# Two token halves chunk by chunk, the tail of a recurrence around a gate's products, and weights split four chunks ahead, in a kernel of eight stages

## The chip, the cores and the metric

The kernel runs on one core of a Trainium2 chip. The metric is the device time of one execution in microseconds (us). Before the change the median of three runs is 1450.25 us (1450.15 to 1452.18). The core's engines work side by side, each through its own list of instructions: TensorE (PE) multiplies matrices, VectorE (DVE), ScalarE (ACT) and GpSimd (POOL) work on tiles of 128 partitions, SyncE (SP) issues most of the transfers.

## The reference

256 tokens of 1024 features pass through two equal layers, each with three branches, and then through a pooling mixer, two convolutional feed-forward stages, two small embedding stages and a sparse attention. The change is in the two layers. One of them, cut to what matters (all in float32):

```python
h = rmsnorm(x, pre_norm_g[l])
proj = h @ w_in[l]
(u, v, z_a, c_q, c_kv, k_rope, z_b, x_c, z_c, g_a, g_b, g_c) = jnp.split(proj, cuts, axis=-1)
y_a = gmlp_spatial(u, v, ...) * jax.nn.silu(z_a)
y_b = mla_attention(c_q, c_kv, k_rope, ...) * jax.nn.silu(z_b)
y_c = rg_lru(x_c, ...) * jax.nn.silu(z_c)
merged = (jax.nn.sigmoid(g_a) * (y_a @ w_proj_a[l])
          + jax.nn.sigmoid(g_b) * (y_b @ w_proj_b[l])
          + jax.nn.sigmoid(g_c) * (y_c @ w_proj_c[l]))
x = x + rmsnorm(merged @ w_out[l], post_norm_g[l])
```

The recurrence of the third branch, `rg_lru`, over 1280 channels:

```python
a = jnp.exp(log_a)
mult = jnp.sqrt(jnp.maximum(1.0 - jnp.exp(2.0 * log_a), 0.0))
bterm = mult * (i * xc)          # h[t] = a[t] * h[t-1] + bterm[t], a scan over the tokens
```

## The kernel before, in words

**Products.** Every float32 product of matrices is made of three: each operand is split into a high part (hi) and a low part (lo), and `mm3` issues hi by hi (line 481), hi by lo (482) and lo by hi (483). Two shapes matter. Where the output is by tokens, the stationary operand is a slice of the activations and the weights stream, 512 columns at a time, for the two halves of 128 tokens one after the other (`tok_halves`, `tok_group`, `tok_pair`). Where it is by features (`feat_tile`, `feat_pair`), 256 tokens stream.

**Weights.** `Stream` (from line 342) brings the weights of the whole program in one sequence of chunks of up to 128 x 1024. SyncE loads a chunk into one of 4 raw buffers, ScalarE copies it to hi (line 376), VectorE subtracts to lo (line 379, in two pieces of 512 columns), and there are 7 buffers for hi and 7 for lo. `get` hands out the next chunk and, by two numbers given at line 428, first writes the loads of the next three chunks and the splits of the next two. A buffer is free again once the last product that reads it is done.

**One layer.** The hidden activations hT are normalised and transposed. The gMLP branch (u, v, za), the attention (c, zb) and the recurrence's input (xc) come first. Then the gates and projections: `gate` makes two halves of 512 columns and takes their tanh on ScalarE into tmp (line 898); `project` makes the product of a branch's y with its projection and adds it to merged on VectorE (lines 907 and 908). `gates` computes the recurrence's decay av (five tiles of 128 x 512, ending in an exponential on ScalarE at line 973) and multiplies its input xc (line 968).

**The tail of the recurrence**, lines 980 to 993: first both column blocks of the third gate (gc 0 and gc 1), then for each of the five tiles the square of av and its minimum with 1 on VectorE (lines 985, 986) and the square root on ScalarE (987), then xc times that (989) and the scan over the tokens (992), two scans for each tile. After it come zc's products, and for each of its five pairs a silu (lines 617 and 618), the product with av (1001) and the split into yc (491 on ScalarE for the high part, 492 on VectorE for the low part). pc's products need yc: for each column block n, half 0 goes through all ten slices of yc, then half 1 does. merged is transposed into ms, multiplied with the output weights (`tok_pair`), normalised (sums of squares as "junk" at 512, ms at 501, rs on GpSimd at 502), and added to x half by half (lines 1016 and 1020); the next stage's norm follows in each half at once (tmp at 526, then transposes, or, at the pool mixer, products with pm at 1089).

**What sets the order.** The code is not a list of each engine's instructions: a scheduler places every instruction on its engine by the order in which it was written and by when buffers come free. An engine then works through its list strictly in that order. So a split that is written earlier can come to stand ahead of an instruction that it has nothing to do with.

Of the kernel before, what the change touches and what calls it, by code (L numbers as in the profile page):

```python
# [418 lines left out]
class Net:  # L419
    def __init__(self, tc, ctx, aps, out):  # L420
        self.tc, self.nc = tc, tc.nc
        self.aps, self.out = aps, out
        self.cp = ctx.enter_context(tc.tile_pool(name="const", bufs=1))
        self.sp = ctx.enter_context(tc.tile_pool(name="stream", bufs=1))
        self.ap = ctx.enter_context(tc.tile_pool(name="acts", bufs=1))
        self.tp = ctx.enter_context(tc.tile_pool(name="temps", bufs=2))
        self.psp = ctx.enter_context(tc.tile_pool(name="psum", bufs=4, space=bass.MemoryType.PSUM))
        self.w = Stream(self.nc, aps["w"], self.sp, 3, 2)

# [136 lines left out]
    def tok_group(self, key, f, N=512, kts=KD, kper=2):  # L566
        return list(self.tok_halves(key, f, N, kts, kper))

# [164 lines left out]
    def first_layer(self, l):  # L733
# [160 lines left out]
        def gate(gk, n):  # L894
            ts = []
            for ps in self.tok_halves((gk, l, n), hT):
                ts.append(self.tmp())
                nc.scalar.activation(ts[-1], ps, AF.Tanh, scale=0.5)
            return ts

        def project(pk, n, y, kts, ts, first=False):
            for half, ps in enumerate(self.tok_halves((pk, l, n), y, kts=kts)):
                mg, t = merged[half][n], ts[half]
# [71 lines left out]
        for kind, i in MERGE_ORDER:  # L975
            if kind == "a":
                project("pa", i, ya, 8, gate("ga", i))
            else:
                gates(i)
        tg = [gate("gc", n) for n in range(2)]  # L980
        tv = self.u2s("tv", 5)
        quarter = self.small(1, "quarter", 2)
        nc.vector.tensor_scalar(quarter, av[4][:, :1], 0.0, 0.25, op0=ALU.mult, op1=ALU.add)
        for j in range(5):
            nc.vector.tensor_tensor(tv[j], av[j], av[j], op=ALU.mult)
            nc.vector.tensor_scalar(tv[j], tv[j], 1.0, None, op0=ALU.min)
            nc.scalar.activation(tv[j], tv[j], AF.Sqrt, bias=quarter, scale=-0.25)
        for j in range(5):
            nc.vector.tensor_tensor(xc[j], xc[j], tv[j], op=ALU.mult)
            for e in range(2):  # L990
                ct = 2 * j + e
                nc.vector.tensor_tensor_scan(ctile(av, ct), ctile(av, ct), ctile(xc, ct), 0.0,  # L992
                                             op0=ALU.mult, op1=ALU.add)
        if l == 1:
            self.ple_load(0)
            self.w.scale = self.row("pscale")
# [8 lines left out]
        for n in range(2):  # L1005
            project("pc", n, yc, KL, tg[n])
        for n in range(2):
# [525 lines left out]
```

## Time and profile before

| | |
|---|---|
| median of three runs | 1450.25 us |
| the profiled execution | 1449.2 us, its span 1447.4 us |
| TensorE busy | 1406.5 us, 97% of the span |
| VectorE busy | 1059.7 us, 73% |
| ScalarE busy | 842.0 us, 58% |
| GpSimd busy | 73.2 us, 5% |
| mean granted TensorE clock | 0.996 of full speed |

The span goes from the first to the last instruction of the profiled execution; 1.8 us of its time lie around the span. Times in the rows further down are in us from the span's start. A row of a timeline has start, duration, engine, line, operation, result and operands, and in square brackets how long the engine had been idle before it and what ended that. Products are pipelined: each is recorded longer than the distance to the next one, so for TensorE the distance between starts is what counts.

### The profile page before, as it was taken

To read this page: it belongs to the slowest core of one execution; us is meant where nothing else is said; L and a number is where in the kernel's file an instruction comes from. 1 tells how busy PE (TensorE), PEld (TensorE's weight loads), DVE (VectorE), ACT (ScalarE), POOL (GpSimd) and SP (SyncE) were. 2 spreads that over 40 slices of the span, in tenths; PEclk is the share of its full clock that TensorE was granted. 3 is DMA by queue.
4 is the path that set the end of the run, shared out by engine and by line. 5 is a ranking of instruction groups with operands and counts; after the bars stand their busy time and mean duration, and the time that the engine had idled before them with its cause. 6 is when DMAs were issued, how large, how long until landed. Compare 5 with 4: busy or idle time off the path is not lost.

```text
span 1447.4 us, 23030 instructions
## 1 busy us (share of the span) xinstructions
PE 1406.5 (97%) x8522; PEld 1235.7 (85%) x8522; DVE 1059.7 (73%) x2163; ACT 842.0 (58%) x1411; POOL 73.2 (5%) x118
## 2 busy tenths in 40 slices
PE   6999999999999999999999999999999999999997
PEld 6987889889789878898897899999778677999986
DVE  7856748659677567486597788776795888787765
ACT  6665545656465665456564566554665786665553
POOL 1000002100010000021000000000100120000000
PEclk9999999999999999999999999999999999999999
DMA  8563456554655634555656455555453106655552
GB/s 281 182 195 117 166 183 196 170 202 149 218 161 195 197 117 159 190 187 170 211 178 218 150 201 178 190 186 193 167 181 131 59 15 191 194 184 189 187 162 90
DMA packets 73408, 249.32 MB, mean 172 GB/s; under 512 B 8272, under 2 KB 8912, under 8 KB 73296
## 3 DMA queue, kind: packets, MB, share of 16 engines
q1 hardware_dynamic: 72576, 245.95, 51.9%
q10 hardware_dynamic: 720, 1.91, 0.4%
q8 instruction: 67, 1.10, 0.3%
q14 instruction: 45, 0.37, 0.1%
HBM read 246.77 MB, written 1.05 MB: 171 GB/s over the span
## 4 chain that ended last, share of the span: by engine, by line
PE 81%; DVE 9%; DMA 4%; ACT 3%; issue 2%; POOL 1%; POOLq 0%; ACTq 0%; DVEq 0%; SPq 0%
PE psA L481 22%; PE psA L482 22%; PE psA L483 22%; DMA raw<-in_w_dram 3%; PE psB L481 3%; PE psB L482 3%; PE psB L483 3%; DVE lo L379 3%; ACT hi L376 2%; PE psB L538 1%; DVE av L992 1%; POOL rs L502 1%; PE psB L1036 1%; PE psB L1054 1%; PE psB L1422 1%
## 5 line engine op out<-in xcount | busy, mean ns | idle before, releaser
L379 DVE TENSOR_TENSOR lo<-raw,hi 128x512 fp32r<-128x512 f32 (+2 forms) x897 | 583.9, 677 | 217.4 <-ACT hi L376 212.0
L376 ACT ACTIVATE hi<-raw 128x1024 fp32r<-128x1024 f32 (+3 forms) x449 | 466.7, 1044 | 310.6 <-PE psA L483 110.3
L482 PE MATMUL psA<-hT,hi 128*128 128x256 f32 x1160 | 328.6, 283 | 0.5 <-DVE hT L489 0.5
L483 PE MATMUL psA<-hT,lo 128*128 128x256 f32 x1160 | 328.2, 283 | 0.0
L481 PE MATMUL psA<-hT,hi 128*128 128x256 f32 x1160 | 328.2, 283 | 0.0
L481 PE MATMUL psA<-hi,hT 128*128 128x512 f32 (+2 forms) x592 | 230.5, 390 | 3.9 <-ACT hT L488 3.9
L482 PE MATMUL psA<-lo,hT 128*128 128x512 f32 (+2 forms) x592 | 228.6, 386 | 1.6 <-DVE lo L379 1.6
L483 PE MATMUL psA<-hi,hT 128*128 128x512 f32 (+2 forms) x592 | 229.1, 388 | 0.0
L482 PEld LDWEIGHTS psA<-hT,hi 128*128 128x128 f32 x1160 | 221.9, 191 | 2.0 <-DVE hT L489 0.7
L481 PEld LDWEIGHTS psA<-hT,hi 128*128 128x128 f32 x1160 | 221.8, 191 | 1.5 <-ACT hT L488 0.2
L483 PEld LDWEIGHTS psA<-hT,lo 128*128 128x128 f32 x1160 | 222.0, 191 | 0.0
L481 PEld LDWEIGHTS psA<-hi,hT 128*128 128x128 f32 x592 | 111.5, 188 | 24.1 <-ACT hT L488 4.9
L482 PEld LDWEIGHTS psA<-lo,hT 128*128 128x128 f32 x592 | 111.4, 188 | 21.9 <-DVE lo L379 2.3
L483 PEld LDWEIGHTS psA<-hi,hT 128*128 128x128 f32 x592 | 111.4, 188 | 20.6 <-DVE hT L489 0.7
L1135 DVE SCALAR_TENSOR_TENSOR tmp<-psA,colt,tmp 128x255 f32<-128x255 f32 (+1 forms) x176 | 84.1, 478 | 1.2
L502 POOL TENSOR_TENSOR rs<-ms,mhalf 128x1 f32<-128x1 f32 x34 | 28.9, 851 | 979.2 <-DVE ms L501 790.6
L481 PE MATMUL psB<-hi,fact 128*128 128x512 f32 x176 | 68.8, 391 | 0.0
L482 PE MATMUL psB<-lo,fact 128*128 128x512 f32 x176 | 68.8, 391 | 0.0
L483 PE MATMUL psB<-hi,fact 128*128 128x512 f32 x176 | 68.5, 389 | 0.0
L1132 ACT ACTIVATE tmp<-psA,colt 128x256 f32<-128x256 f32 x88 | 48.5, 551 | 1.9
L512 ACT ACTIVATE junk<-x 128x512 bf16<-128x512 f32 x36 | 22.6, 628 | 36.3 <-DVE x L1165 14.0
L936 POOL CAST es<-xs 64x256 fp32r<-64x256 f32 x48 | 29.4, 640 | 270.1 <-ACT xs L488 269.3
(343 smaller groups left out, 2235.0 us busy)
## 6 DMA issues: line engine op xcount, KB each, us to landing
raw<-in_w_dram SPq DMA_DIRECT2D x414, 512.0 KB, 3.7
raw<-in_w_dram SPq DMA_DIRECT2D x24, 384.0 KB, 3.9
row<-in_rows_dram SPq DMA_DIRECT2D x34, 256.0 KB, 5.6
raw<-in_w_dram SPq DMA_DIRECT2D x8, 448.0 KB, 3.2
raw<-in_w_dram SPq DMA_DIRECT2D x4, 480.0 KB, 3.3
x<-in_x_dram SPq DMA_DIRECT2D x4, 256.0 KB, 4.6
pm<-in_pm_dram ACTq DMA_DIRECT2D x2, 512.0 KB, 5.3
out_dram<-h SPq DMA_DIRECT2D x4, 256.0 KB, 2.1
```

Of the source, the lines that this page charges most:

```text
L376: self.nc.scalar.activation(hi[:, :n], t[:, :n], AF.Copy)
L379: self.nc.vector.tensor_tensor(lo[:, c], t[:, c], hi[:, c].bitcast(F32), op=ALU.subtract)
L481: mm(ps, a[0], b[0], start=start, stop=False)
L482: mm(ps, a[0], b[1], start=False, stop=False)
L483: mm(ps, a[1], b[0], start=False, stop=stop)
L502: nc.gpsimd.tensor_tensor(rs, ms, self.mhalf, op=ALU.pow)
L512: nc.scalar.activation(junk[:, :s.shape[1]], s, AF.Square, scale=float(n) ** -0.5 / mul, accum_out=ss[:, i:i + 1])
L538: nc.tensor.transpose(ps[:, i, :], src[:, (done + i) * P:(done + i + 1) * P], self.cf("ident"))
L936: nc.gpsimd.tensor_copy(edges[p][m][i][r], xs.pair(ct)[i][r].bitcast(F32))
L992: nc.vector.tensor_tensor_scan(ctile(av, ct), ctile(av, ct), ctile(xc, ct), 0.0, op0=ALU.mult, op1=ALU.add)
L1132: nc.scalar.activation(dst, src, AF.Identity, bias=self.col("fb", ct, l), scale=self.col("fw", 2 * 2 * KF + ct, l))
L1135: nc.vector.scalar_tensor_tensor(dst[:, s:], src[:, :S - s], self.col("fw", (2 - s) * 2 * KF + ct, l), dst[:, s:], op0=ALU.mult, op1=ALU.add)
```

## The change

The diff has four parts. `Stream` gets 6 and 4 in place of 3 and 2. `tok_group`, which was a list of what `tok_halves` yields, now takes a chunk of weights, does its products for half 0 and for half 1, and only then takes the next; both sums are complete at the end. `gate` uses it, and so does `project`, except for pc's second column block. And the tail of the recurrence is written anew: squares on ScalarE, minima on GpSimd, square roots, then gc 0, then products and scans, then gc 1.

```diff
-        self.w = Stream(self.nc, aps["w"], self.sp, 3, 2)
+        self.w = Stream(self.nc, aps["w"], self.sp, 6, 4)
...
     def tok_group(self, key, f, N=512, kts=KD, kper=2):
-        return list(self.tok_halves(key, f, N, kts, kper))
+        ps = [self.psA(), self.psA()]
+        for c in range(-(-kts // kper)):
+            wh, wl = self.w.get((*key, c), N)
+            for half in range(2):
+                for kg in range(c * kper, min(kts, (c + 1) * kper)):
+                    k = kg % kper
+                    self.mm3(ps[half][:, :N], f.pair(kg, half), (wh[:, k, :], wl[:, k, :]), kg == 0, kg == kts - 1)
+        return ps
...
         def gate(gk, n):
             ts = []
-            for ps in self.tok_halves((gk, l, n), hT):
+            for ps in self.tok_group((gk, l, n), hT):
...
-        def project(pk, n, y, kts, ts, first=False):
-            for half, ps in enumerate(self.tok_halves((pk, l, n), y, kts=kts)):
+        def project(pk, n, y, kts, ts, first=False, last=False):
+            for half, ps in enumerate((self.tok_halves if last else self.tok_group)((pk, l, n), y, kts=kts)):
...
-        tg = [gate("gc", n) for n in range(2)]
         tv = self.u2s("tv", 5)
         quarter = self.small(1, "quarter", 2)
         nc.vector.tensor_scalar(quarter, av[4][:, :1], 0.0, 0.25, op0=ALU.mult, op1=ALU.add)
         for j in range(5):
-            nc.vector.tensor_tensor(tv[j], av[j], av[j], op=ALU.mult)
-            nc.vector.tensor_scalar(tv[j], tv[j], 1.0, None, op0=ALU.min)
+            nc.scalar.activation(tv[j], av[j], AF.Square)
+            nc.gpsimd.tensor_scalar(tv[j], tv[j], 1.0, 1.0, op0=ALU.min, op1=ALU.mult)
+        for j in range(5):
             nc.scalar.activation(tv[j], tv[j], AF.Sqrt, bias=quarter, scale=-0.25)
+        tg = [gate("gc", 0)]
         for j in range(5):
             nc.vector.tensor_tensor(xc[j], xc[j], tv[j], op=ALU.mult)
             for e in range(2):
...
+        tg.append(gate("gc", 1))
...
         for n in range(2):
-            project("pc", n, yc, KL, tg[n])
+            project("pc", n, yc, KL, tg[n], last=(n == 1))
```

All lines from 566 on move down by 7, those behind the tail by 9: line 618 of before is 625 of after, 1016 is 1025.

The order in which engines get their instructions changes with it at three places. The first is ScalarE in layer 0, from the gates of the recurrence to the first silu of zc. Before (tmp at 967 are the gates' last tanh, at 898 the third gate's, tv at 987 the square roots):

```order
L967 ACTIVATE tmp<-psA,lrub_717 128x256 x3
L376 ACTIVATE hi<-raw 128x1024 x2
L898 ACTIVATE tmp<-psA 128x512
L376 ACTIVATE hi<-raw 128x1024 x3
L898 ACTIVATE tmp<-psA 128x512
...
L987 ACT_TABLE_LOAD
L987 ACTIVATE tv<-tv,quarter 128x512 x5
```

and now (squares at 991, square roots at 994, the third gate's tanh at 905):

```order
L974 ACTIVATE tmp<-psA,lrub_733 128x256 x3
L991 ACTIVATE tv<-av 128x512 x5
L994 ACT_TABLE_LOAD
L994 ACTIVATE tv<-tv,quarter 128x512 x5
L376 ACTIVATE hi<-raw 128x1024 x3
L905 ACT_TABLE_LOAD
L905 ACTIVATE tmp<-psA 128x512 x2
L376 ACTIVATE hi<-raw 128x1024 x4
```

The square roots have moved ahead of the third gate's tanh, and three splits that stood ahead of that tanh now stand behind the square roots.

The second is VectorE in the same stretch, from the last xc of the gates on. Before (the tail is lines 985 to 992; a scan is listed as an operation of av and xc):

```order
L968 SCALAR_TENSOR_TENSOR xc<-tmp,xc 128x256 x3
L379 TENSOR_TENSOR lo<-raw,hi 128x512 x18
L985 TENSOR_TENSOR tv<-av 128x512 x2
L986 TENSOR_SCALAR tv<-tv 128x512 x2
...
L989 TENSOR_TENSOR xc<-xc,tv 128x512 x2
L992 SCALAR_TENSOR_TENSOR av<-av,xc 128x256 x4
L618 SCALAR_TENSOR_TENSOR tmp<-tmp,psA 128x512
```

and now (products at 997, scans at 1000):

```order
L975 SCALAR_TENSOR_TENSOR xc<-tmp,xc 128x256 x3
L379 TENSOR_TENSOR lo<-raw,hi 128x512
L997 TENSOR_TENSOR xc<-xc,tv 128x512 x2
L1000 SCALAR_TENSOR_TENSOR av<-av,xc 128x256 x4
L997 TENSOR_TENSOR xc<-xc,tv 128x512 x2
L379 TENSOR_TENSOR lo<-raw,hi 128x512 x6
L1000 SCALAR_TENSOR_TENSOR av<-av,xc 128x256 x4
L997 TENSOR_TENSOR xc<-xc,tv 128x512
L379 TENSOR_TENSOR lo<-raw,hi 128x512
L1000 SCALAR_TENSOR_TENSOR av<-av,xc 128x256 x2
L379 TENSOR_TENSOR lo<-raw,hi 128x512 x16
L625 SCALAR_TENSOR_TENSOR tmp<-tmp,psA 128x512
```

The 18 splits that stood ahead of the tail now mostly stand behind it, and none of its squares and minima is left.

The third is VectorE at the end of layer 1, where x is updated half by half (x_70 is half 0, x_71 half 1), and the pool mixer's rows are scaled (tmp). Before:

```order
L501 TENSOR_SCALAR ms<-ss 128x1
L1020 SCALAR_TENSOR_TENSOR x_70<-t,rs,x_70 128x512 x2
L501 TENSOR_SCALAR ms<-ss 128x1
L526 SCALAR_TENSOR_TENSOR tmp<-x_70,rs,row 128x512 x2
L1016 TENSOR_TENSOR t<-psA,row 128x512 x2
```

and now:

```order
L501 TENSOR_SCALAR ms<-ss 128x1
L1029 SCALAR_TENSOR_TENSOR x_70<-t,rs,x_70 128x512
L379 TENSOR_TENSOR lo<-raw,hi 128x512 x4
L1029 SCALAR_TENSOR_TENSOR x_70<-t,rs,x_70 128x512
L501 TENSOR_SCALAR ms<-ss 128x1
L526 SCALAR_TENSOR_TENSOR tmp<-x_70,rs,row 128x512 x2
L1025 TENSOR_TENSOR t<-psA,row 128x512 x2
```

Four splits have come between the two updates of half 0. On TensorE the order at the three places is the same as before, but for the order of halves within a product.

## Rows read from the trace of the kernel before

**Rows 1.** The page's first part: busy time of each engine, its share of the span, and instructions.

```profile
PE 1406.5 (97%) x8522; PEld 1235.7 (85%) x8522; DVE 1059.7 (73%) x2163; ACT 842.0 (58%) x1411; POOL 73.2 (5%) x118
```

**Rows 2.** The waits of TensorE over the whole span: the operation that waited, what it waited for, us in total, times, the longest.

```profile
PE psB L538 <- DVE tmp L526: 12.6, 5, 9.6
...
PE psA L481 <- ACT yc L491: 3.3, 3, 1.7
...
PE psA L482 <- DVE lo L379: 1.6, 2, 1.3
...
PE psA L483 <- DVE yc L492: 0.8, 2, 0.4
```

**Rows 3.** The timeline of TensorE in layer 0, at pc's first product and at the end of the first half's eighth slice.

```profile
356.57 0.40 PE L481 MATMUL psA<-hi,yc 128*128 128x512 f32 x1
...
361.58 0.39 PE L482 MATMUL psA<-lo,yc 128*128 128x512 f32 x1
361.81 0.39 PE L483 MATMUL psA<-hi,yc 128*128 128x512 f32 x1
363.85 0.50 PE L481 MATMUL psA<-hi,yc 128*128 128x512 f32 x1 [1.66 <-ACT yc L491]
364.19 0.40 PE L482 MATMUL psA<-lo,yc 128*128 128x512 f32 x1
365.00 0.50 PE L483 MATMUL psA<-hi,yc 128*128 128x512 f32 x1 [0.41 <-DVE yc L492]
```

**Rows 4.** The same in layer 1; of the stretch from 758.13 to 767.90 only the ends and the place between its two parts.

```profile
755.61 0.40 PE L481 MATMUL psA<-hi,yc 128*128 128x512 f32 x1
...
758.13 0.39 PE L483 MATMUL psA<-hi,yc 128*128 128x512 f32 x1
...
763.56 0.57 PE L481 MATMUL psA<-hi,yc 128*128 128x512 f32 x1
...
767.90 0.39 PE L481 MATMUL psA<-hi,yc 128*128 128x512 f32 x1
```

**Rows 5.** Windows of the span: length, then busy us and instructions of PE, PEld, DVE, ACT, POOL, then the granted TensorE clock, the share of the DMA engines, GB/s.

```profile
764.00:767.00 3.00, 3.00 (x9) 2.33 (x8) 1.66 (x3) 0.63 (x1) 0.00 (x0) 0.50 0.77 264
...
822.00:825.00 3.00, 3.00 (x15) 3.00 (x16) 2.66 (x5) 1.16 (x3) 0.00 (x0) 0.50 0.88 261
```

**Rows 6.** The timeline of VectorE in layer 0, in the recurrence's tail and behind it.

```profile
328.36 1.29 DVE L985 TENSOR_TENSOR tv<-av 128x512 f32<-128x512 f32 x2
329.57 0.76 DVE L986 TENSOR_SCALAR tv<-tv 128x512 f32<-128x512 f32 x2
...
339.56 2.42 DVE L992 TENSOR_TENSOR_SCAN av<-av,xc 128x256 f32<-128x256 f32 x4
341.91 0.65 DVE L618 SCALAR_TENSOR_TENSOR tmp<-tmp,psA 128x512 f32<-128x512 f32 x1
...
364.26 0.68 DVE L492 SCALAR_TENSOR_TENSOR yc<-tmp,yc 128x512 fp32r<-128x512 f32 x1
```

**Rows 7.** The timeline of ScalarE in the same stretch: the table load ahead of the square roots, and one of the splits among the silus.

```profile
329.54 1.28 ACT L987 ACT_TABLE_LOAD   x1
...
346.59 1.06 ACT L376 ACTIVATE hi<-raw 128x1024 fp32r<-128x1024 f32 x1 [1.61 <-DMA raw<-in_w_dram]
```

**Rows 8.** The timeline of VectorE in layer 1: the low part of yc's fifth pair.

```profile
765.66 0.69 DVE L492 SCALAR_TENSOR_TENSOR yc<-tmp,yc 128x512 fp32r<-128x512 f32 x1 [0.70 <-ACT yc L491]
```

**Rows 9.** The timeline of VectorE in layer 0's gMLP branch: the last steps of v's norm.

```profile
115.10 1.30 DVE L869 TENSOR_TENSOR sv<-sv,row 128x512 f32<-128x512 f32 x2
116.32 1.28 DVE L870 TENSOR_TENSOR sv<-sv,row 128x512 f32<-128x512 f32 x2
```

**Rows 10.** The timeline of TensorE there: the products that read them.

```profile
122.84 1.46 PE L873 MATMUL psB<-sv,wsT 128*128 128x256 f32 x6
```

**Rows 11.** The timeline of ScalarE in layer 0: the last tanh of the recurrence's gates.

```profile
306.36 1.21 ACT L967 ACTIVATE tmp<-psA,lrub 128x256 f32<-128x256 f32 x3
```

**Rows 12.** The page's groups of instructions: the squares that ScalarE does for the norms; count, busy us, mean ns of one, idle time before.

```profile
L512 ACT ACTIVATE junk<-x 128x512 bf16<-128x512 f32 x36 | 22.6, 628 | 36.3 <-DVE x L1165 14.0
```

**Rows 13.** GpSimd's instructions by line and shape: count, busy us, mean ns of one, idle time before and what ended it.

```profile
L1412 POOL TENSOR_SCALAR es<-es,sm 128x256 f32<-128x256 f32 x16 | 8.5, 550 | 24.7 <-PE psB L1422 8.0 <-DVE sm L1408 7.9 <-PE psA L1399 6.2
L1412 POOL TENSOR_SCALAR es<-es,sm 128x128 f32<-128x128 f32 x16 | 6.2, 403 | 95.8 <-DVE sm L1408 95.8
```

**Rows 14.** The timeline of VectorE in layer 0, during gc 0 and gc 1.

```profile
314.11 4.02 DVE L379 TENSOR_TENSOR lo<-raw,hi 128x512 fp32r<-128x512 f32 x6 [2.89 <-ACT hi L376]
...
325.04 3.41 DVE L379 TENSOR_TENSOR lo<-raw,hi 128x512 fp32r<-128x512 f32 x5 [5.07 <-ACT hi L376]
```

**Rows 15.** The timeline of VectorE at the end of layer 1.

```profile
809.05 1.42 DVE L1020 SCALAR_TENSOR_TENSOR x<-t,rs,x 128x512 f32<-128x512 f32 x2 [0.73 <-POOL rs L502]
811.31 0.21 DVE L501 TENSOR_SCALAR ms<-ss 128x1 f32<-128x1 f32 x1 [0.85 <-ACT junk L512]
812.19 1.42 DVE L526 SCALAR_TENSOR_TENSOR tmp<-x,rs,row 128x512 f32<-128x512 f32 x2 [0.66 <-POOL rs L502]
...
820.96 1.41 DVE L526 SCALAR_TENSOR_TENSOR tmp<-x,rs,row 128x512 f32<-128x512 f32 x2 [0.45 <-POOL rs L502]
```

**Rows 16.** The timeline of TensorE there: the pool mixer's products for half 1.

```profile
821.76 2.93 PE L1089 MATMUL psB<-pm,tmp 128*128 128x128 f32 x12 [2.71 <-DVE tmp L526]
```

**Rows 17.** The waits of TensorE from 366 to 430 us, at the step from layer 0 to layer 1.

```profile
PE psB L538 <- DVE tmp L526: 1.2, 2, 0.8
```

## The prediction

> **What bounds the kernel now.** I read the page's busy line first, then TensorE's waits, then the timelines around the places where the diff works, and the order of instructions last. TensorE is busy for 1406.5 of the span's 1447.4 us [rows 1], so only what shortens its waits or lifts its clock can shorten the run: nothing in the diff adds or takes away a matrix product. The list of its waits [rows 2] splits them by what came last. Weights are a small part: the wait for a low part of a split weight (DVE lo) is 1.6 us in all, 1.3 of it in one piece. What can be won by a change to the first layers is the wait for yc: 3.3 us for its high part, 0.8 for its low part. The largest entry, 12.6, is mostly one wait of 9.6 us at the start, which the diff doesn't touch.
>
> The reader should see the place of the yc wait in the two timelines. In layer 0 [rows 3] products of 512 columns start every 0.227 us (361.58, 361.81, and 24 of them from 356.57 on); then come 2.04, 0.34 and 0.81 us instead of three times 0.227: 3.19 - 0.68 = 2.5 us lost. In layer 1 [rows 4] ten steps from 758.13 to 763.56 take 5.43 instead of 2.27: 3.2 us lost. Right after it the granted clock of 764 to 767 is 0.50, the lower of the two levels [rows 5]. There the twelve steps from 763.56 to 767.90 take 4.34 instead of 2.72: 1.6 us more. Together **7.3 us** hang on yc in the two layers.
>
> Why is yc late? In layer 0, pc's first product starts at 356.57, and half 0 runs through eight of its ten slices before it needs the fifth pair, 24 x 0.227 = 5.4 us later. The fifth pair's low part starts on VectorE at 364.26. Ahead of it stands VectorE's tail of the recurrence: from 328.36 to 341.9 it does squares, minima, products and scans without one lo among them, and the silu of the first pair waits until 341.91 [rows 6].
>
> **Part 1, products chunk by chunk (tok_group).** For pc with n = 0 both halves of a chunk now run together: the fifth pair is wanted after 48 products instead of 24, 10.9 us after the start instead of 5.4. In layer 0 that is 367.5, against 364.94 at which the low part was done even in the kernel before [rows 6]; 2.5 us to spare. In layer 1 pc starts at 755.61 [rows 4], so the pair is wanted at 766.5; its low part ended at 765.66 + 0.69 = 766.35 [rows 8], 0.15 us to spare. So this part alone already removes the wait of layer 0 and nearly that of layer 1: -2.5 and -3.2, and, with no wait ahead of it, I take the 1.6 of slow clock with them. What it costs: half 0's sums come 5.4 us later than before, together with half 1's. For the gates that is free, since their tanh is used only by project. In the gMLP branch the normalised v must be there for the products with wsT: VectorE has it at 116.32 + 1.28 = 117.6, TensorE starts at 122.84 [rows 9, 10], 5.2 us later. The second half's chain, some 3 to 4 us of VectorE work (four of 0.64 in the same rows, and the statistics), now follows the first's instead of lying 5.4 us behind it; it still fits. I take 0, with 0 to +2 for each layer as bounds.
>
> **Part 2, the recurrence's tail.** Five multiplications of 0.60 and five minima of 0.34 [rows 6] leave VectorE, 4.7 us; the rest of the tail moves ahead, between gate 0's and gate 1's products. Who is loaded instead? ScalarE's last tanh of the gates ends at 307.57 [rows 11]. Five squares of 512 columns: the nearest row, the same function, is 0.63 us each with about 0.53 from start to start [rows 12], so they end near 310.2; the table load of 1.28 [rows 7] ends at 311.5. GpSimd has no 512-column row. The same operation takes 403 ns at 128 columns and 550 at 256 [rows 13]: 147 ns for each 128 more gives 0.84 us. Bounds are 0.55 (no more than at 256) and 1.5 (some way beyond twice the longer row, 1.1). With 0.84 the last minimum ends at 308.1 + 4.2 = 312.3, the last square root near 314.3. VectorE had two holes there, 2.9 us before 314.11 and 5.1 before 325.04 [rows 14]; the products and scans (five of 0.6, ten of 0.59, 8.9 us) now lie around them. What must not be late is the second chunk of gate 1, wanted at about 319.7 (gate 0 ends at 316.9, one chunk is 2.7): its hi now stands behind the five square roots, and its lo behind four products and four scans. I get its lo at about 318.4, 1.3 us to spare. So no wait, and the recurrence ends near 325 instead of 341.9. That makes the fifth yc ready some 3.5 to 5 us after zc instead of 8.5, which widens part 1's spare to 5 us and covers layer 1. No further term: the 7.3 are not won twice.
>
> The Trainium skill speaks against the move: ScalarE: Activation LUTs, "Rules for kernel authors", wants mul and min on VectorE, which it puts at up to about three times faster per element in bf16. By that a square would be 3 x 0.60 = 1.8 us, an estimate from that page, the five would end at 316.5, gate 1's second chunk would come some 0.4 us late in each layer, and the forecast would be 0.8 us higher. The float rows here are 0.63 against 0.68 [rows 6, 12], so I don't take it.
>
> **Part 3, weights four ahead (6, 4).** The order shows the limit: seven hi and lo buffers and four raw ones. Ahead of zc's first silu ScalarE has issued only three more hi than before. With 1.6 us of weight waits in the whole run [rows 2]: 0, bounds -0.3 and +0.5. But the splits are now written earlier, so the scheduler puts them elsewhere among the norm chains, and there VectorE pays.
>
> At the step from layer 1 to the pool mixer, VectorE's two updates of x for half 0 were one group at 809.05; ms follows at 811.31, the scaled rows (tmp) at 812.19, then half 1's t and x, and its tmp at 820.96 [rows 15]. TensorE waits for that last tmp, 2.71 us until 821.76 [rows 16]. In the new order four lo stand between the two updates, 4 x 0.60 = 2.4 us, and ScalarE has two hi ahead of half 0's sums of squares. Everything in half 0's chain is one behind the other, with 0.85 and 0.66 us of idle time that wait on its own links, so the delay runs through: half 1's t, which VectorE takes only after half 0's tmp, comes 2.4 later, and so does the wait's end. TensorE has no other work in its order there: **+2.3**. Bounds: 0, if the lo fall into VectorE's idle time, and +3.8, if TensorE then runs 3 us longer at the lower level, as it does after this wait now (822 to 825 at 0.50, [rows 5]), which costs another 1.5. At the step between the layers two more lo come ahead of half 0's ms in the same way; there the transposes waited 1.2 us in two pieces for tmp [rows 17]. +0.3, bounds -0.5 and +1.2.
>
> **The sum.** -2.5 - 3.2 - 1.6 + 2.3 + 0.3 = -4.7 us. The profiled run took 1449.2 us (span 1447.4, 1.8 around it): 1444.5. The median of the three runs is 1450.25, 1.05 above the profiled one; the forecast in that measure is **1445.5**, 0.3% faster. Own range 1443.0 to 1447.5. A measurement of this kernel tells about 0.2%, 2.9 us, from no change.
>
> **Rivals.**
> A, nothing is given back: the lo fall into idle time at both steps. Then -7.3, 1443.0. For it: VectorE idles in short pieces all around 809 to 817 [rows 15]. Against: these are links of the same chain.
> B, yc stays late, the change doesn't free it: the fifth pair is held not by VectorE but by weights. ScalarE does hi and tmp in one order, and there each hi waits for its raw load, up to 1.6 us a time [rows 7]. If weights read further ahead push yc back by more than 2.5 us in layer 0, or by more than 0.15 in layer 1 with no gain from the tail, most of the wait returns; with half of 7.3 left, -3.6 + 2.6 = -1.0, 1449.2: no change.
> C, slower: GpSimd's minimum is much slower than its shorter rows. ScalarE's square roots wait for it, three hi behind them, and TensorE waits in gate 1 for its second chunk. It decides from about 1.7 us for one minimum (five of them, then square root, hi and two lo before 319.7). At 3 us it is 5 x 1.3 = 6.5 us late in each layer: -4.7 + 13 = +8.3, 1458.5; at 2.2 it evens the gain out, 1450. At 128 and 256 columns it stays under 0.56 us in the mean, which speaks against it.
> D, slower as well: chunk by chunk costs more than part 1 says, the gMLP chain misses its 5.2 us by 2 in each layer and TensorE's clock falls after it (1.5 each): -4.7 + 7 = +2.3, 1452.5.
>
> **Chances.** Forecast 0.50, A 0.16, B and other small sums 0.22, C 0.05, D 0.07. Faster by over 0.2%: 0.66, within: 0.22, slower: 0.12. For 8 in 10 the range goes from below A, 1441.0, for bounds that all fall well, past B to just short of D, 1452.0.
>
> **What would show it.** In the profile after: no wait of TensorE for yc, and pc with 0.227 us steps through, in both layers; clock 1.00 where it was 0.50 in layer 1. GpSimd's five minima at 0.7 to 0.9 us. The last scan before 327 in layer 0's old times. TensorE's wait at the pool mixer near 5 us instead of 2.7. Wrong, if TensorE waits for hi or lo within gate 1 (C), for yc (B), at wsT (D), or if the pool mixer's wait is unchanged (A).

## The result and the profile after

The changed kernel takes 1457.16 us (median of 4 runs, 1455.19 to 1457.94) against 1450.2 before: ratio 1.0052, 95% interval 1.0039 to 1.0065. It is slower by about 7 us, where 5 us less were forecast. Its profiled execution took 1455.19 us, span 1453.4 us, 6.0 more than the span before. Two of e1's six executions, the profiled one among them, were disturbed (1541 us, with the clock at 0.85, and 5539 us) and aren't counted; e14 is the same kernel with another profile.

Busy time by engine [rows 1]:

```profile
PE 1409.3 (97%) x8522; PEld 1237.2 (85%) x8522; DVE 1051.3 (72%) x2143; ACT 845.5 (58%) x1421; POOL 91.9 (6%) x128
```

VectorE and ScalarE have nearly the load of before; GpSimd has 18.7 us more, and only ten instructions did that. TensorE's waits over the span [rows 2] tell where the time is, and where it is no more: no line has yc in it.

```profile
PE psB L538 <- DVE tmp L526: 14.5, 6, 9.8
PE psB L1098 <- DVE tmp L526: 5.0, 2, 4.8
...
PE psA L481 <- ACT hi L376: 2.1, 2, 1.0
...
PE psA L482 <- DVE lo L379: 1.3, 4, 0.5
```

**The yc wait is gone**, as forecast, and with it the slow clock of layer 1: the window of [rows 5], whose clock was 0.50, is at 1.00 (columns as there). But the second one, after the pool mixer's wait, has become longer: 0.50 for 826 to 830, and 0.84 for the 5 us behind. The recurrence ends earlier, as part 2 reckoned: the fifth pair of yc is complete 5.4 us after pc's first product in layer 0 and 6.3 in layer 1, where it was 8.4 and 10.8 before.

```profile
764.00:767.00 3.00, 3.00 (x15) 2.50 (x14) 2.90 (x5) 1.98 (x3) 0.00 (x0) 1.00 0.85 224
...
826.00:830.00 4.00, 3.88 (x18) 3.88 (x19) 1.99 (x5) 0.00 (x0) 0.00 (x0) 0.50 0.82 269
830.00:835.00 5.00, 4.78 (x34) 4.57 (x34) 3.05 (x5) 3.34 (x7) 0.00 (x0) 0.84 0.04 13
```

**Gate 1 waits**, which it didn't before. ScalarE's timeline in layer 0 begins as reckoned: five squares in 2.74 us, about 0.5 each and not the 1.8 of the estimate that the prediction set aside, and the table loaded by 311.9. Then the square roots wait for GpSimd, the last three about 1.5 us each (idle times in brackets), and the hi for gate 1 begin at 320.12; on TensorE's timeline gate 1's second chunk is late:

```profile
307.82 2.74 ACT L991 ACTIVATE tv<-av 128x512 f32<-128x512 f32 x5
...
315.14 0.72 ACT L994 ACTIVATE tv<-tv,quarter 128x512 f32<-128x512 f32 x1 [1.49 <-POOL tv L992]
317.31 0.72 ACT L994 ACTIVATE tv<-tv,quarter 128x512 f32<-128x512 f32 x1 [1.45 <-POOL tv L992]
319.49 0.72 ACT L994 ACTIVATE tv<-tv,quarter 128x512 f32<-128x512 f32 x1 [1.46 <-POOL tv L992]
320.12 2.94 ACT L376 ACTIVATE hi<-raw 128x1024 fp32r<-128x1024 f32 x3
```

```profile
319.79 0.39 PE L483 MATMUL psA<-hi,hT 128*128 128x512 f32 x1
321.21 0.51 PE L481 MATMUL psA<-hi,hT 128*128 128x512 f32 x1 [1.03 <-ACT hi L376]
321.94 0.51 PE L482 MATMUL psA<-lo,hT 128*128 128x512 f32 x1 [0.22 <-DVE lo L379]
```

The reason, in GpSimd's instructions by shape [rows 13]: the new line takes 2186 ns where 840 were reckoned from the two below it.

```profile
L992 POOL TENSOR_SCALAR tv<-tv 128x512 f32<-128x512 f32 x10 | 21.6, 2186 | 91.9 <-ACT tv L991 91.9
L1421 POOL TENSOR_SCALAR es<-es,sm 128x256 f32<-128x256 f32 x16 | 8.0, 518 | 25.2 <-PE psB L483 8.9 <-DVE sm L1417 7.7 <-PE psA L1408 6.2
L1421 POOL TENSOR_SCALAR es<-es,sm 128x128 f32<-128x128 f32 x16 | 6.0, 394 | 97.0 <-DVE sm L1417 97.0
```

**The pool mixer's start.** VectorE [rows 15], now with four lo between the updates of x, and a second hole further on:

```profile
808.63 0.75 DVE L1029 SCALAR_TENSOR_TENSOR x<-t,rs,x 128x512 f32<-128x512 f32 x1 [0.68 <-POOL rs L502]
809.31 2.49 DVE L379 TENSOR_TENSOR lo<-raw,hi 128x512 fp32r<-128x512 f32 x4
811.71 0.74 DVE L1029 SCALAR_TENSOR_TENSOR x<-t,rs,x 128x512 f32<-128x512 f32 x1
...
814.19 1.41 DVE L526 SCALAR_TENSOR_TENSOR tmp<-x,rs,row 128x512 f32<-128x512 f32 x2 [0.66 <-POOL rs L502]
...
820.27 0.21 DVE L501 TENSOR_SCALAR ms<-ss 128x1 f32<-128x1 f32 x1 [2.27 <-ACT junk L512]
...
825.32 1.41 DVE L526 SCALAR_TENSOR_TENSOR tmp<-x,rs,row 128x512 f32<-128x512 f32 x2 [0.44 <-POOL rs L502]
```

Half 0's tmp is 2.0 us later than before (814.19 for 812.19), the delay that the four lo explain; half 1's is 4.4 later (825.32 for 820.96). In between, ScalarE stands still at the third of three hi, and half 1's sum of squares (junk) behind it:

```profile
813.18 2.00 ACT L376 ACTIVATE hi<-raw 128x1024 fp32r<-128x1024 f32 x2
818.03 1.06 ACT L376 ACTIVATE hi<-raw 128x1024 fp32r<-128x1024 f32 x1 [2.85 <-PE psB L1098]
818.99 0.58 ACT L512 ACTIVATE junk<-psA 128x512 bf16<-128x512 f32 x1
```

The profile puts that wait down to a product; but the hi needs its raw chunk, whose load was issued at 810.65 and landed at 817.94, just ahead of the hi at 818.03. Of the five raw loads issued between 805 and 820 two took 7.3 us to land, the other three 3.2 to 3.3. In that stretch the mixer's own matrix pm (queue q10) took its share of the transfer engines, 48.4% against 38.8% for the weights, from 810 to 818:

```profile
q10 hardware_dynamic: 288, 1.05, 48.4%
q1 hardware_dynamic: 354, 1.27, 38.8%
...
raw<-in_w_dram SPq DMA_DIRECT2D x2, 512.0 KB, 7.3
pm<-in_pm_dram ACTq DMA_DIRECT2D x1, 512.0 KB, 6.9
```

A raw load met pm before the change too: issued at 808.26, it took 6.5 us and landed at 814.77. But then its hi stood behind half 1's first two sums of squares, and nothing was held:

```profile
814.30 0.60 ACT L512 ACTIVATE junk<-psA 128x512 bf16<-128x512 f32 x1 [0.17 <-DVE t L1016]
...
815.49 1.05 ACT L376 ACTIVATE hi<-raw 128x1024 fp32r<-128x1024 f32 x1
```

So what is new is the order on ScalarE. The new order also delays pm itself, which ScalarE issues: it now stands behind two more hi and a sum of squares, its second transfer is issued at 809.90 instead of 807.54 and lands at 816.75 instead of 813.54. On TensorE three waits that weren't there before come ahead of the one for half 1's tmp. The profile puts the second down to VectorE's t; it ends at 816.89, right behind the landing of pm. The third is for uf, the mixer's first products, which ScalarE splits only at 820.13, behind the held hi and the two sums of squares:

```profile
815.04 1.13 PE L1098 MATMUL psB<-pm,tmp 128*128 128x128 f32 x8 [0.16 <-DVE tmp L526]
816.89 2.92 PE L1098 MATMUL psB<-pm,tmp 128*128 128x128 f32 x24 [0.71 <-DVE t L1025]
820.78 0.39 PE L481 MATMUL psA<-hi,uf 128*128 128x256 f32 x1 [0.97 <-ACT uf L488]
```

**The whole, by stage.** The table has what TensorE lost in each profiled execution: for each product the distance from its start to the next one's start, less the usual distance for its shape (0.227 us at 512 columns, 0.120 at 256), summed over the products of a stage. It counts waits and slow clock alike. Spans differ by these sums to within 0.6. The column of layer 1 reaches to the first product with the output weights (about 1 us in every run), that of the mixer to the first products of the next stage. Each row is one execution, up to 2 us off the median of its kernel.

| us lost | gc 0 and gc 1, both layers | zc and pc, layer 0 | zc and pc, layer 1 | output product of layer 1 to the mixer | all else | sum |
|---|---|---|---|---|---|---|
| before | 0.0 | 2.6 | 6.0 | 7.3 | 45.4 | 61.3 |
| after | 3.6 | 0.0 | 0.9 | 13.2 | 49.3 | 67.0 |
| e2, minima on VectorE | 0.0 | 0.0 | 1.0 | 13.1 | 50.6 | 64.7 |
| e3, only 6 and 4 | 0.0 | 5.5 | 5.0 | 12.3 | 46.6 | 69.4 |
| e4, only the tail | 14.4 | 0.0 | 1.2 | 7.3 | 44.4 | 67.3 |
| e5, minima on VectorE, 3 and 2 | 1.0 | 0.0 | 1.0 | 7.4 | 49.1 | 58.5 |
| e6, only chunk by chunk | 0.0 | 0.0 | 1.1 | 7.4 | 47.6 | 56.1 |
| e7, only pc by chunks | 0.0 | 0.0 | 2.5 | 9.1 | 44.5 | 56.1 |
| e9, only 6 and 2 | 0.0 | 5.1 | 6.8 | 5.8 | 43.3 | 61.0 |
| e10, pc by chunks and tail on VectorE | 8.3 | 0.0 | 1.0 | 7.3 | 42.6 | 59.2 |
| e13, gates and projections by chunks | 0.0 | 0.0 | 0.9 | 5.8 | 45.5 | 52.2 |
| e14, the change with 3 and 2 | 10.2 | 0.0 | 1.0 | 7.2 | 49.9 | 68.3 |
| e15, e13 and tail on VectorE | 1.0 | 0.0 | 0.9 | 5.7 | 44.9 | 52.5 |

So the change won 7.7 us at yc and lost 3.6 in the gates, 5.9 at the mixer and 3.9 elsewhere: +5.7 of the span's +6.0.

### The profile page after: what moved, and what is told of

Its sections match the earlier page's. It is cut to its first block, busy times and chain, and to the rows that moved or that the text cites. A ratio compares the mean times of both kernels' runs of the same rounds, so it can differ in the third digit from the quotient of the medians.

```text
span 1453.4 us, 23061 instructions
## 1 busy us (share of the span) xinstructions
PE 1409.3 (97%) x8522; PEld 1237.2 (85%) x8522; DVE 1051.3 (72%) x2143; ACT 845.5 (58%) x1421; POOL 91.9 (6%) x128
## 4 chain that ended last, share of the span: by engine, by line
PE 84%; DVE 5%; ACT 4%; DMA 2%; issue 2%; POOL 2%; POOLq 0%; ACTq 0%; DVEq 0%; SPq 0%
PE psA L482 22%; PE psA L483 22%; PE psA L481 22%; PE psB L481 3%; PE psB L482 3%; PE psB L483 3%; DMA raw<-in_w_dram 2%; DVE lo L379 2%; ACT hi L376 2%; POOL tv L992 1%; PE psB L538 1%; POOL rs L502 1%; PE psB L1045 1%; PE psB L1063 1%; PE psB L1058 1%
## 5 line engine op out<-in xcount | busy, mean ns | idle before, releaser
L1141 ACT ACTIVATE tmp<-psA,colt 128x256 f32<-128x256 f32 x88 | 48.4, 550 | 1.9
```

Of the source, the lines that this page charges most:

```text
L1141: nc.scalar.activation(dst, src, AF.Identity, bias=self.col("fb", ct, l), scale=self.col("fw", 2 * 2 * KF + ct, l))
```

## The experiments

My theory after the two traces: GpSimd's slow minima hold gate 1's splits, and splits four ahead stand in the mixer's norm chain. The first rival: chunk by chunk is what delays the chains.

**e1 and e14, the change with 3 and 2.**

```diff
-        self.w = Stream(self.nc, aps["w"], self.sp, 6, 4)
+        self.w = Stream(self.nc, aps["w"], self.sp, 3, 2)
```

> The changed kernel with the weights' numbers back at 3 and 2; everything else of the change stays. My theory, from the two traces: of the change's +6.0 us in the profiled runs the pool mixer's start is +5.9 (a wait of 4.84 us for tmp instead of 2.71, and a longer stretch at the lower clock), and its cause is the splits that are written four chunks ahead and then stand among half 0's norm chain on VectorE and ScalarE. It expects the two updates of x for half 0 as one group again, a wait of about 2.7 us there, and about 6 us less than the changed kernel: 1450 to 1451, ratio to before 1.000 to 1.001. Rival 1, that sums which come chunk by chunk are late for the norm chains: the wait at the pool mixer stays near 4.8 and the time near 1456 to 1457.

1455.9 us, ratio 1.0045 (1.0029 to 1.006): not what my theory expected, and near what its rival did.

> The changed kernel with 3 and 2 once more, for a profile. Its earlier time was 1455 to 1458 where 1450 was expected. Theory A: with splits written only two ahead gate 1's chunks are fewer ahead when ScalarE is held by GpSimd's minima, and TensorE waits 4 us or more a layer in gate 1 instead of 1.8; the pool mixer's wait is 2.7. Theory B: the waits in gate 1 are as in the changed kernel and the pool mixer's wait is near 4.8.

1456.27 us, ratio 1.004 (1.0027 to 1.0054), and its profile is theory A's: the mixer's loss is back at 7.2, and the gates lose 10.2 us instead of 3.6. TensorE's waits in layer 0 from 305 to 335 us:

```profile
PE psA L482 <- DVE lo L379: 2.2, 3, 1.1
PE psA L481 <- ACT hi L376: 1.0, 1, 1.0
```

With 6 and 4 ScalarE does three hi right behind the square roots, with 3 and 2 only two, then a table load and two tanh, and the third comes later. In layer 0 the clock also fell behind that wait (0.50 from 328.7 to 332), which it didn't in the changed kernel. So splits further ahead, a loss at the mixer, soften the loss in the gates: the two parts hide each other, and my first theory had taken their costs as independent. That part of it fell.

**e2, minima on VectorE.**

```diff
-            nc.gpsimd.tensor_scalar(tv[j], tv[j], 1.0, 1.0, op0=ALU.min, op1=ALU.mult)
+            nc.vector.tensor_scalar(tv[j], tv[j], 1.0, None, op0=ALU.min)
```

> The changed kernel with the five minima on VectorE (as before the change) instead of GpSimd; squares stay on ScalarE, 6 and 4 stay. My theory: GpSimd took 10.81 us for five minima, 2.16 each where 0.84 was reckoned, the square roots waited for it, the weights' splits stood behind the square roots, and TensorE lost 1.85 us in gate 1 of each layer. It expects no wait in gate 1, 3.7 us less than the changed kernel: 1453 to 1454, ratio 1.002 to 1.003. Rival: ScalarE's extra squares and table loads alone hold the splits: then the waits in gate 1 stay above 1 us a layer and the time within 1.5 us of the changed kernel.

1453.11 us, ratio 1.0024 (1.0015 to 1.0033). No wait in the gates; the squares and table loads on ScalarE hold nothing. GpSimd's minima cost the 3.6 us of the table, 4 by the medians.

**e3, only 6 and 4**, the reverse of the first diff, in the kernel before.

> The kernel before with the weights' numbers 6 and 4 alone. My theory: it takes the loss at the pool mixer by itself, with the updates of x for half 0 apart and a wait for tmp of about 4.8 us there; +5 to +7 against before: 1455 to 1457, ratio 1.0035 to 1.005. The yc waits stay as before. Rival 1 (chunk by chunk is to blame): no change, 1450, ratio within 0.1%.

1458.12 us, ratio 1.0061 (1.0046 to 1.0076), slower than expected. As expected in place: the same four lo between the updates of x, the same wait for tmp at the mixer, 4.8 us, 12.3 us lost there. I hadn't expected 2.9 us more to be lost at layer 0's yc; a part of them is the clock, at 0.50 from 366.6 to 369.9, where it was 1.00 before.

```profile
813.50 2.49 DVE L379 TENSOR_TENSOR lo<-raw,hi 128x512 fp32r<-128x512 f32 x4
```

```profile
PE psB L1089 <- DVE tmp L526: 4.8, 1, 4.8
```

**e9, only 6 and 2**, to tell the loads from the splits.

> The kernel before with the weights' numbers 6 and 2: loads six ahead, splits two ahead as before. My theory: the loss of the run with 6 and 4 alone (+5.05 us at the pool mixer, +2.9 at layer 0's yc) comes from the splits being written four ahead, which puts them among the norm chain, and four raw buffers leave the number of loads without effect. No change: 1448 to 1451, ratio 0.999 to 1.001. Rival: loads that are issued earlier collide with other transfers (pm at the pool mixer) by themselves: +4 or more, 1453 and above.

1448.84 us, ratio 0.9994 (0.9985 to 1.0003): no change, and 5.8 us lost at the mixer. The number of splits does it. yc moved here too, by 2.5 us in layer 0 with the same stretch of slow clock, without a change of the time as a whole: e3's 2.9 there don't need splits four ahead.

**e4, only the tail**, with gates and projections by halves, 3 and 2.

```diff
-        tg = [gate("gc", n) for n in range(2)]
...
-            nc.vector.tensor_tensor(tv[j], av[j], av[j], op=ALU.mult)
-            nc.vector.tensor_scalar(tv[j], tv[j], 1.0, None, op0=ALU.min)
+            nc.scalar.activation(tv[j], av[j], AF.Square)
+            nc.gpsimd.tensor_scalar(tv[j], tv[j], 1.0, 1.0, op0=ALU.min, op1=ALU.mult)
...
+        tg = [gate("gc", 0)]
...
+        tg.append(gate("gc", 1))
```

> The kernel before with the new tail alone (squares on ScalarE, minima on GpSimd, gate 0 and gate 1 around the products); 3 and 2, and halves one after the other. My theory: the recurrence ends earlier, yc is on time or nearly (up to -7.3 us), but in gate 1 half 0 wants all four chunks within 5.4 us, so the splits held behind GpSimd's minima cost more than in the changed kernel: a wait of 3 to 4 us in each layer. Together -1 to +1: 1449 to 1451. Rival: the late splits also delay yc, whose waits stay: +5, 1455.

1455.56 us, ratio 1.0042 (1.0028 to 1.0055), slower than I expected; the rival's time, but not its cause. yc is on time by the tail alone (0.0 and 1.2 us), but the gates lose 14.4 us, a stretch of 0.50 clock behind the wait in each layer among them: by halves, the first half wants all four chunks at once.

**e6, only chunk by chunk**, the new `tok_group` with the old tail, 3 and 2.

> The kernel before with chunk by chunk alone (gates, projections, v, u, za; not pc's second block); old tail, 3 and 2. My theory: layer 0's yc wait goes with 2.5 us to spare and layer 1's with 0.15, so -6 to -7.4, and 2 to 4 us come back in the attention of both layers and at the step between them, since half 0's sums come 5.4 us later: 1445 to 1448, ratio 0.997 to 0.9985. Rival 1: layer 1's spare of 0.15 doesn't hold and some of its wait stays, 1449. Rival 2 (chunk by chunk costs nothing): 1442 to 1443, ratio 0.995.

1445.58 us, ratio 0.9974 (0.9963 to 0.9984), as my theory expected. The yc wait is gone in both layers with the old tail. Beside it 2.2 us are lost elsewhere. One of its new waits, in the sparse attention (TensorE's waits from 1040 to 1200 us; the stretch before the change has none of this line):

```profile
PE psB L1363 <- DVE qs L489: 1.4, 1, 1.4
```

**e7, only pc's first block by chunks** (`tok_chunks` has the body of the new `tok_group`; every other use stays by halves).

```diff
-            project("pc", n, yc, KL, tg[n])
+            project("pc", n, yc, KL, tg[n], chunks=(n == 0))
```

> The kernel before with chunk by chunk in one place alone, pc's first column block in each layer; everything else as before, also every other use of halves. My theory: the yc wait goes in layer 0, and in layer 1 but for what 0.15 us of spare can't cover; nothing else moves by more than a few splits: -6 to -7.4, 1442 to 1444, ratio 0.995 to 0.996. Rival: the scheduler places splits anew and some norm chain loses 3 or more: 1446 and above.

1442.89 us, ratio 0.9953 (0.9941 to 0.9966). This one place, in each layer, wins what the change was to win. The spare of 0.15 us in layer 1 did not hold: two waits for yc, 0.31 and 0.41 us, at 764.

**e13, gates and projections by chunks**, every other user of `tok_group` by halves, old tail, 3 and 2.

```diff
-            for ps in self.tok_halves((gk, l, n), hT):
+            for ps in self.tok_chunks((gk, l, n), hT):
...
-            for half, ps in enumerate(self.tok_halves((pk, l, n), y, kts=kts)):
+            for half, ps in enumerate((self.tok_halves if last else self.tok_chunks)((pk, l, n), y, kts=kts)):
```

> The kernel before with chunk by chunk for the gates and the projections alone (not pc's second block); v, u, za, pp and the sparse attention's queries, keys and values by halves as before; old tail, 3 and 2. My theory: the 2 to 4 us that chunk by chunk everywhere gives back (against -7.4 won) come from those other users, whose first half is wanted at once by a norm or a transpose: 1441 to 1443.5, ratio 0.9945 to 0.996, and TensorE's lost time in the first attention and in the sparse attention as before. Rival: they come with the gates and projections: no better than chunk by chunk everywhere, 1445 to 1446.5.

1440.35 us, ratio 0.9934 (0.992 to 0.9948), below what I expected, and the fastest of all with e15. Windows of its trace (columns as in [rows 5]): no idle TensorE in layer 0 from 300 to 370, and at the mixer no slow clock.

```profile
300.00:330.00 30.00, 30.00 (x167) 26.24 (x166) 19.24 (x35) 20.16 (x31) 0.00 (x0) 1.00 0.60 202
330.00:370.00 40.00, 40.00 (x285) 37.80 (x284) 38.61 (x67) 25.70 (x32) 0.00 (x0) 1.00 0.51 176
...
800.00:850.00 50.00, 45.44 (x332) 42.26 (x331) 41.76 (x75) 33.41 (x59) 4.42 (x6) 1.00 0.59 197
```

Against e6 it differs in the other users alone (v, u, za, pp, and the sparse attention's queries, keys and values), and takes 5.2 us less by the medians, 3.9 in the table. 1.6 of these are the slow clock at the mixer, which e13 doesn't have behind the same wait of 2.7 us; why is not shown. By the measure of the table e6 loses 2.7 more in the stretches of the two layers where v, u and za run among the attention's heads, and 1.1 more in the sparse attention, and less in some other places: chunk by chunk costs there. That a norm or a transpose waits for half 0 is shown for one place alone, the qs above.

**e15, e13 with the tail around gate 1**, squares on ScalarE, minima on VectorE.

> The run before last (gates and projections by chunks, 3 and 2) with the tail around gate 1 as well, squares on ScalarE and minima on VectorE. My theory: once the halves run together the yc wait is gone without the tail, so the tail adds nothing but half a microsecond to a microsecond of wait in gate 1 of each layer: 0 to +1.5 us against chunk by chunk without the tail, 1442 to 1445. Rival: the tail frees VectorE later on and gains 1 us or more: below 1441.5.

1441.18 us, ratio 0.9934 (0.992 to 0.9947). The same as e13: 1.0 us lost in the gates, 0.6 less elsewhere. Once the halves of pc run together the tail's place is worth nothing.

**e10, pc's first block by chunks and the tail on VectorE**, gates by halves.

> The kernel before with the two parts that have paid so far: chunk by chunk for pc's first block alone, and the tail written around gate 1 with squares on ScalarE and minima on VectorE; gates by halves, 3 and 2. My theory: the 1.2 us of yc wait that pc by chunks alone leaves in layer 1 goes, no wait comes in gate 1 since the square roots end near 315 and half 0 wants its last chunk near 321; 1 to 2 us less than with pc alone, 1441 to 1442.5, ratio 0.994 to 0.995. Rival: with halves gate 1 wants its chunks sooner than in the changed kernel and waits 1 to 3 us a layer for splits held behind the square roots: 1444 to 1448, no better than pc alone or worse.

1447.93 us, ratio 0.999 (0.9981 to 0.9999). The rival's: 8.3 us lost in the gates, a stretch of 0.50 clock behind the wait in each layer among them, and 5 more than pc alone by the medians. VectorE's scans now stand ahead of the lo that half 0 of gate 1 wants. TensorE's waits in layer 0 from 305 to 335 us:

```profile
PE psA L482 <- DVE lo L379: 2.2, 2, 1.9
```

**e5, the change with minima on VectorE, and 3 and 2.**

> The changed kernel with the minima on VectorE and the weights' numbers back at 3 and 2: what is left of the change is chunk by chunk, the squares on ScalarE and the new place of the tail. My theory, with the terms of the runs so far: no wait in gate 1, no yc wait (-7.4), no loss at the pool mixer, and 2 to 4 us lost in the attention and norm chains of both layers, where chunk by chunk delivers half 0 later: 1445 to 1448, ratio 0.997 to 0.9985. Rival, that waits at the pool mixer come with chunk by chunk after all (the run with 3 and 2 alone left the time at +0.45%): 1452 to 1453, ratio 1.002.

1448.11 us, ratio 0.9997 (0.9988 to 1.0006): the mixer's loss is gone, as my theory said, but time and ratio are just above what it expected; 3.7 us more than before lie in "all else", where e6 has 2.2 more and e14 4.5.

**e8, e11 and e12, GpSimd's operation by itself**, in the changed kernel: one operation instead of two; two operations on half the columns; a product with a column instead of the minimum, which this kernel leaves out, at 512 columns. One execution each.

```diff
-            nc.gpsimd.tensor_scalar(tv[j], tv[j], 1.0, 1.0, op0=ALU.min, op1=ALU.mult)
+            nc.gpsimd.tensor_scalar(tv[j], tv[j], 1.0, None, op0=ALU.min)
```

> The changed kernel with GpSimd's minimum written as one operation (min with 1) instead of two (min with 1, times 1). Theory A: 2.16 us each is what a pass of 512 columns with two operations takes there, where the rows of the kernel before (403 and 550 ns) had one: now 0.8 to 0.9 each, no wait in gate 1. Theory B: the operation's count doesn't matter, and 512 columns or the constant operand make it 2.2 again; the wait in gate 1 stays at 1.8 us a layer.

> The changed kernel with each of GpSimd's minima (two operations) cut into two of 256 columns. Tells what the rows of the kernel before were worth as a measure. Theory A, time goes with columns times operations: 1.1 us each, 10 in 11 us a layer, as long as before. Theory B, passes of 512 columns are slow for their length: 0.55 each, 5.5 us a layer, and no wait in gate 1.

> The changed kernel with GpSimd's minimum replaced by a product with a per-partition column (so the recurrence's square root gets another argument: this part of the computation is changed), the operation of the rows 403 and 550 ns, at 512 columns. Theory A, the length decides: 1.6 us, as the minimum as one operation took. Theory B, the minimum with a constant is the slow one: 0.8 to 0.9 us.

GpSimd's rows, of e8, e11 and e12:

```profile
L992 POOL TENSOR_SCALAR tv<-tv 128x512 f32<-128x512 f32 x10 | 16.3, 1658 | 91.9 <-ACT tv L991 91.9
```

```profile
L993 POOL TENSOR_SCALAR tv<-tv 128x256 f32<-128x256 f32 x20 | 24.1, 1233 | 91.9 <-ACT tv L991 91.9
```

```profile
L992 POOL TENSOR_SCALAR tv<-tv,quarter 128x512 f32<-128x512 f32 x10 | 17.7, 1786 | 91.9 <-ACT tv L991 91.9
```

Neither theory of e8 holds: one operation takes 1.66, between 0.85 and 2.2, so the second one adds 0.5. The wait in gate 1 is gone, at 1450.24 us. e12's product takes 1.79, and there is no wait in gate 1 either (1451.05 us): the wait begins between 1.79 and 2.16, not at the 1.7 that the prediction reckoned. e11 is nearer theory A's: half the columns, a little more than half the time, 1464.32 us, and the wait is longer.

The expectations of e8 and e12 have one thing wrong. The operation of [rows 13] is not one but two: line 1412 multiplies by a column and then by 1.0. So at 256 columns, with two operations each, the product there takes 0.52 us and e11's minimum 1.23. The rows that were extended were of other arithmetic in another place, and neither the length nor the number of operations explains the difference; which of the two, arithmetic or place, does is open. VectorE's work beside GpSimd explains only a part: the second minimum of the changed kernel, beside a VectorE that worked for 0.26 us, still took 1.92.

## Why the prediction was wrong

**The chain and its cover were right.** The yc wait went in both layers, and the slow clock behind it: -7.7 us in the table for -7.3. Chunk by chunk does it alone (e6, e7), as part 1 said; in layer 1 the spare of 0.15 us was too thin by some tenths in e7.

**Part 2's "so no wait" fell by its price.** The step was 0.84 us for a minimum, extended from two rows of shorter shapes, with 1.5 as upper bound. It is 2.16 from start to start. The prediction called those rows "the same operation", but they are products, in another place; e11 shows that the minimum takes more than twice as long at one of their lengths already. Rival C had the mechanism and the place, and a point of decision, 1.7, that was near (none at 1.79, a wait at 2.16), but a chance of 5 in 100; at 2.2 us it priced 2.5 us a layer, and 1.8 are lost. e2 shows it by taking the minima away from GpSimd, e8 by making them shorter.

**Part 3's +2.3 at the mixer had the right cause and too small a size**: +5.9. The delay of half 0's chain was 2.0 us, near the 2.4 reckoned. But "the delay runs through" left out what else the splits hold on ScalarE. One hi waits for a raw chunk whose load meets pm's transfer, with half 1's sums of squares and uf queued behind it, and pm is issued later: half 1's tmp comes 4.4 us later instead of 2.4, and TensorE has three new waits of 1.8 us in all before it. The wait for tmp itself came out as forecast, near 5, by luck: it is 2.1 longer only because TensorE gets there later too. And it is followed by a longer stretch at the lower clock, about 1 us more, which stood only as +1.5 in the bound. That the splits are the cause is shown (e3 and e9); that pm's transfer is what delays the raw chunk is read from the transfers and wasn't tried by moving pm.

**Part 1's cost of 0 was wrong**, though where I looked it held: the product with wsT doesn't wait. What loses is the attention of both layers, among whose heads v, u and za run, and less the sparse attention (e6 against e13); in the changed kernel the two layers have 2.7 of the 3.9 us that it loses elsewhere. D's mechanism, then, in other places, at less than its price and without its slow clock.

**The step between the layers** was to cost 0.3, at most 1.2. By the measure of the table it cost 1.4. The wait for tmp there [rows 17] went from 1.2 to 2.7 us; it is 1.8 with 6 and 4 alone (e3) and 1.2 with 3 and 2 (e6, e14): once more the splits four ahead.

**The sum** then reads -7.7 + 3.6 + 5.9 + 3.9 = +5.7 where -4.7 was forecast: three terms of cost, each with its mechanism named and each priced too low. The range of 1441 to 1452 let one of them go wrong at a time.

## What to carry to other kernels

A change that moves work to another engine is first priced there by a row of the same shape; where there is none, the range has to hold a multiple of any extension from shorter ones, and the point from which the engine behind it is late decides the chance, not the mean. A row is of the same operation only if its arithmetic is the same too, and that stands in the code, not in the profile's line. Splitting further ahead is no free lead where buffers limit it: here it put such work ahead of a chain that it has nothing to do with, and helped only where another part had made the splits late (e14). And the part that pays should be tried by itself: running the two halves of a product together where its operand comes late won all (e7, e13), and the other parts gave nothing or cost.

## What the runs showed of the hardware that was not expected

GpSimd's elementwise passes over float tiles of 128 partitions differ widely in price. In the tail a minimum with a constant at 512 columns takes 1.66 as one operation and 2.19 with a product with 1.0 as the second (e8, after), and 1.23 at 256 with two (e11); a product with a column takes 1.79 at 512 as one operation (e12). In the sparse attention a product with a column and with 1.0 takes 0.39 at 128 columns and 0.52 at 256. Arithmetic and place differ between the two, and which of them is the cause is not shown. The same minimum on VectorE is 0.34 [rows 6].

Side by side the two engines both took longer: in e12 GpSimd's second product took 1.56 us with VectorE idle, its fourth 2.18 beside four scans on VectorE, and those took 3.25 us instead of the 2.42 of [rows 6].

After a wait of 2.71 us at the mixer TensorE ran at 0.50 of its clock for about 3 us [rows 5], after one of 4.84 for 4 and part of the next 5, and in e13 and e9, whose waits there are 2.7 again, not at all.
